# Ten quads of MLP down products as seven block products each, in a two-layer decoder trunk on one core

## The chip, the cores and the metric

The kernel runs on one core of a Trainium2 chip. The metric is the device time of one execution in microseconds. A profiled execution carries its own time beside its span (the time from the first to the last instruction that the profile holds).

## What is computed

The reference is a trunk of two layers on 512 tokens of width 1024, all in float32. In each layer the mixing part (attention, a short convolution, RWKV-7) comes first and is not touched here. Then comes the MLP:

```
h = rms_norm(x, norm_mlp_g[l])                              # x: (512, 1024)
x = x + square(relu(h @ w_mlp_up[l])) @ w_mlp_down[l]       # up: 1024 -> 4096, down: 4096 -> 1024
```

After the second layer there is a last norm. Only the MLP's two products matter below.

## The kernel before

Activations lie transposed, feature rows on the 128 partitions and the 512 tokens in the free dimension; `x[0..7]` are the eight residual tiles of 128x512. Every float32 product is made of three passes on TensorE (PE): each operand is split into a high part (a rounded copy, cast by ScalarE, ACT) and a low part (the difference, a subtraction on VectorE, DVE, or GpSimd, POOL), and the passes are high·high, low·high and high·low. So each weight tile costs one load, one cast on ACT (`whi`, `shi`) and one subtraction on DVE (`wlo`, `slo`).

**Up.** The up product has 32 groups of 128 hidden columns. Four (`up`) are plain. The other 28 go in 14 calls of `two(i0, i1)`, each of which makes two groups with seven block products in place of eight, by a scheme of the Strassen-Winograd kind: weights are cut into blocks of 4x128 rows, tokens into halves of H = 256, and four sums of weight blocks (`s1` to `s4`, DVE), four sums of activation blocks (`th`, made once in a layer by `blocks`) and a few sums of results replace one product. One product is 4 blocks by 3 passes, 12 matmuls of 256 columns. Results lie in PSUM banks `pa`, `pb`, `pc`; ACT copies some out (`p1`, `p5`, `u2`, `c1`), DVE adds. `square` makes the hidden tile (relu times the token's norm, then the square), and `kept` splits it into `mh` (ACT) and `ml` (POOL, from the fifth tile on) and adds it to the list `mids`.

**Down.** `down(h, js)` multiplies four hidden tiles (index h, 0 to 7) by the weights of four output tiles j (js is 0 to 3 or 4 to 7): per j 4x3 = 12 matmuls of 512 columns into a bank `dn`, and an addition of the bank to `x[j]` on DVE. `weights` loads, casts and subtracts; it has three sets of buffers in the pool `wp`, and every fourth tile uses a set in `fp` (`spare`).

The loop over p = 0 to 13 calls `two`, and as soon as four tiles more are there, one `down` of four products. So the steady state is an alternation of one `two` and one `down` of four j, called a unit below. The order of instructions on each engine is made by a list scheduler when the program is built; each engine then works in that order, and waits where an operand or a buffer isn't ready.

In layer 0 all of h = 0 to 7 goes through `down`; in layer 1 h = 6 and 7 go through `last_group`.

Of the kernel before, what the change touches and what calls it, by code (L numbers as in the profile page):

```python
# [22 lines left out]
S = 512  # L23
# [159 lines left out]

WHOLE = 5
# [87 lines left out]
def tile_trunk(ctx: ExitStack, tc: tile.TileContext, xT, wts, prm_d, cst_d, lora_d, gup_d, lam_d, fin_d, hd_d, out):  # L272
# [46 lines left out]
    fixed = cp.tile([P, 9], F32, tag="ones1", name="ones1")  # L319
# [246 lines left out]
    for l in range(L):  # L566
# [826 lines left out]
        with ExitStack() as mx:  # L1393
            fp = mx.enter_context(tc.tile_pool(name=f"fp{l}", bufs=1))
            spare[0] = fp
# [6 lines left out]
            def kept(m):  # L1402

                i = len(mids)
                hi = fp.tile([P, S], F32R, tag="mh", bufs=RING, name=f"mh{l}_{i}")
                lo = fp.tile([P, S], F32R, tag="ml", bufs=RING, name=f"ml{l}_{i}")
                act.copy(hi, m)  # L1407
                (dve if i < 4 else pool).tensor_tensor(lo, m, hi.bitcast(F32), ALU.subtract)  # L1408
                mids.append((hi, lo))

            def square(cs, name):

                r = fp.tile([P, S], F32, tag="r", bufs=2, name=f"r{name}")
# [5 lines left out]
                kept(m)  # L1419

# [25 lines left out]
            def blocks(q):  # L1446
                hi, lo = th[q] = [fp.tile([P, 4, H], F32R, tag=f"t{p}{q}", name=f"t{p}{l}_{q}") for p in ("hi", "lo")]
                for i in range(2):
                    u = slice(2 * i, 2 * i + 2)
                    t = fp.tile([P, 2, H], F32, tag="c0" if q == 1 else ("s3", "s4")[i], bufs=1 + (q == 1), name=f"t{l}_{q}_{i}")  # L1450
                    for k in (2 * i, 2 * i + 1):
                        b1, b2, o = bn[k], bn[k + 4], t[:, k % 2]
                        if q == 0:
                            dve.tensor_tensor(o, b1[:, 1], b1[:, 0], ALU.subtract)
                        elif q == 1:
                            dve.tensor_tensor(o, b2[:, 1], tb[0, i][:, k % 2], ALU.subtract)
                        elif q == 2:
                            dve.tensor_tensor(o, b2[:, 1], b1[:, 1], ALU.subtract)
                        else:
                            dve.tensor_tensor(o, b2[:, 0], tb[1, i][:, k % 2], ALU.subtract)  # L1460
                    tb[q, i] = t
                    act.copy(hi[:, u], t)
                    dve.tensor_tensor(lo[:, u], t, hi[:, u].bitcast(F32), ALU.subtract)

            def two(i0, i1):
# [4 lines left out]
                def raw(i, a):  # L1470
                    t = fp.tile([P, 4, P], F32, tag="sraw", bufs=6, name=f"raw{n}_{i}_{a}")
                    nc.sync.dma_start(t.rearrange("p k c -> p (k c)"), wts[wg + i, :, a * P:(a + 4) * P])
                    return t
# [7 lines left out]
                def sum_(name, a, b, op):  # L1481
                    t = fp.tile([P, 4, P], F32, tag=name, name=f"{name}{n}")
# [27 lines left out]
                w21 = raw(i1, 0)  # L1510
                w22 = raw(i1, 4)
                s1 = sum_("s1", w21, w22, ALU.add)
# [3 lines left out]
                s2 = sum_("s2", s1, w11, ALU.subtract)  # L1516
# [3 lines left out]
                w12 = raw(i0, 4)  # L1520
                product(pc, both(w12, "p2"), blk(1, 0))
                dve.tensor_tensor(c0[:, :H], pc, p1, ALU.add)
                s3 = sum_("s3", w11, w21, ALU.subtract)
# [4 lines left out]
                s4 = sum_("s4", w12, s2, ALU.subtract)  # L1528
                product(pb, both(s4, "p3"), blk(1, 1), False)
                dve.tensor_tensor(c0[:, H:], pb, u2, ALU.add)  # L1530
                square([c0], f"{n}_0")
                product(pa, both(w22, "p4"), smm(3), False)
                square([pa, c1], f"{n}_1")

            def down(h, js):

                g, k0 = h // 2, 4 * (h % 2)
# [29 lines left out]
            for p in range(N_TWO):  # L1567
                two(N_ONE + p, N_ONE + N_TWO + p)
                if len(mids) >= 4 * h + 6 and h < 2 * N_KG - 2 * (l == L - 1):
                    down(h, range(4 * half, 4 * half + 4))  # L1570
                    h, half = h + half, 1 - half
            while h < 2 * N_KG - 2 * (l == L - 1):
                down(h, range(4 * half, 4 * half + 4))
                h, half = h + half, 1 - half
# [71 lines left out]
```

## Time and profile before

| | us |
|---|---|
| median of 3 runs | 1236.49 (1235.99 to 1236.52) |
| profiled execution, its own time | 1238.42 |
| its span | 1236.6 |
| PE busy | 1226.2 (99%) |
| DVE busy | 934.4 (76%) |
| ACT busy | 693.0 (56%) |
| POOL busy | 351.7 (28%) |
| TensorE clock granted | 0.998 of full |

The profiled execution took 1.93 us more than the median, and its span is 1.8 us shorter than its own time. "Busy" is the time in which an engine had at least one instruction in work. The share of PE is nearly the whole span, so what matters is how far the matmuls stand apart in a stage, and which wait would come last there if PE had less to do.

### The profile page before, as it was taken

What the parts mean: (1) busy time and instruction counts of PE and PEld (TensorE: products, weight loads), DVE (VectorE), ACT (ScalarE), POOL (GpSimd) and SP (SyncE); (2) the same over time, 40 slices, a digit from 0 to 9 for tenths busy, and PEclk for the clock granted to TensorE, in tenths of its full rate; (3) what the DMA queues carried; (4) which work ended last, traced back from release to release, by engine and by line L of the source; (5) the groups of instructions that cost most, each with busy time, mean ns of one, the idle gap of its engine ahead of it and who ended that gap; (6) DMA issues with size and microseconds to landing.
All of it is one profiled execution on the core that took longest, in us unless ns stands there. A gap on an engine that the chain in (4) does not pass through costs nothing.

```text
span 1236.6 us, 25555 instructions
## 1 busy us (share of the span) xinstructions
PE 1226.2 (99%) x9730; PEld 1056.4 (85%) x9730; DVE 934.4 (76%) x1805; ACT 693.0 (56%) x1456; POOL 351.7 (28%) x450
## 2 busy tenths in 40 slices
PE   9999999999999999999999999999999999999997
PEld 7788788888999998989888888888889999998987
DVE  6787888879887676765666777887798867676753
ACT  6785655558455454544465657464775545454542
POOL 2263636341122111120035455464202211111111
PEclk9999999999999999999999999999999999999999
DMA  6523323124433323321235243232433333323121
GB/s 217 165 91 96 111 90 111 54 86 154 143 97 102 103 94 107 99 86 44 69 105 166 77 126 114 88 85 70 152 113 118 106 102 102 104 95 107 55 69 68
DMA packets 84266, 127.94 MB, mean 103 GB/s; under 512 B 21296, under 2 KB 25136, under 8 KB 84144
## 3 DMA queue, kind: packets, MB, share of 16 engines
q1 hardware_dynamic: 83424, 125.57, 32.5%
q8 instruction: 76, 1.25, 0.4%
q10 hardware_dynamic: 720, 0.75, 0.2%
q14 instruction: 46, 0.38, 0.1%
HBM read 117.11 MB, written 9.18 MB: 102 GB/s over the span
## 4 chain that ended last, share of the span: by engine, by line
PE 92%; DVE 2%; ACT 2%; DMA 1%; POOL 1%; issue 1%; SPq 0%; POOLq 0%; ACTq 0%; DVEq 0%
PE dn L285 25%; PE pj L285 21%; PE pa L285 13%; PE po L285 8%; PE pb L285 7%; PE dnF L285 4%; PE pc L285 3%; PE up L285 2%; PE sc L285 1%; PE ptt L290 1%; PE pg L285 1%; PE pyy L285 1%; PE pzw L285 1%; PE pst L285 1%; DMA raw<-wts 0%
## 5 line engine op out<-in xcount | busy, mean ns | idle before, releaser
L1408 POOL TENSOR_TENSOR ml<-m,mh 128x512 fp32r<-128x512 f32 x56 | 90.5, 1634 | 497.5 <-ACT mh L1407 356.5
L285 PE MATMUL dn<-mh,whi 128*128 128x512 f32 x448 | 175.5, 392 | 0.0
L285 PE MATMUL dn<-ml,whi 128*128 128x512 f32 x448 | 175.2, 391 | 0.1
L285 PE MATMUL dn<-mh,wlo 128*128 128x512 f32 x448 | 175.2, 391 | 0.0
L692 POOL TENSOR_TENSOR wlo<-raw,whi 128x512 fp32r<-128x512 f32 x84 | 111.5, 1328 | 210.4 <-ACT whi L680 167.2
L346 ACT CAST whi<-raw 128x512 fp32r<-128x512 f32 x126 | 77.9, 619 | 157.5 <-PE dn L285 147.8
L285 PE MATMUL pj<-ahim,whi 128*128 128x512 f32 x392 | 156.8, 400 | 0.0
L285 PE MATMUL pj<-ahim,wlo 128*128 128x512 f32 x392 | 156.4, 399 | 0.0
L285 PE MATMUL pj<-alom,whi 128*128 128x512 f32 x392 | 155.9, 398 | 0.0
L1554 DVE TENSOR_TENSOR x<-dn,x 128x512 f32<-128x512 f32 x108 | 74.5, 690 | 89.9 <-PE dn L285 89.8
L680 ACT CAST whi<-raw 128x512 fp32r<-128x512 f32 x142 | 87.7, 618 | 71.7 <-PE pj L285 27.5
L1477 ACT CAST shi_p<-s 128x512 fp32r<-128x512 f32 x112 | 69.4, 621 | 78.4 <-PE pa L285 61.9
L347 DVE TENSOR_TENSOR wlo<-raw,whi 128x512 fp32r<-128x512 f32 x126 | 97.3, 774 | 6.1 <-ACT whi L346 6.1
L285 PEld LDWEIGHTS dn<-mh,wlo 128*128 128x128 f32 x448 | 84.2, 188 | 18.5
L285 PEld LDWEIGHTS dn<-ml,whi 128*128 128x128 f32 x448 | 84.2, 188 | 17.7 <-DVE ml L1408 0.5
L285 PEld LDWEIGHTS dn<-mh,whi 128*128 128x128 f32 x448 | 84.1, 188 | 17.4
L285 PE MATMUL pa<-thi,shi_p 128*128 128x256 f32 x336 | 95.1, 283 | 0.0
L285 PE MATMUL pa<-tlo,shi_p 128*128 128x256 f32 x336 | 94.9, 282 | 0.0
L285 PE MATMUL pa<-thi,slo_p 128*128 128x256 f32 x336 | 94.1, 280 | 0.0
L1478 DVE TENSOR_TENSOR slo_p<-s,shi_p 128x512 fp32r<-128x512 f32 x112 | 77.6, 697 | 21.2 <-ACT shi_p L1477 18.4
L285 PEld LDWEIGHTS pj<-alom,whi 128*128 128x128 f32 x392 | 73.9, 188 | 14.0 <-issue 0.5
L285 PEld LDWEIGHTS pj<-ahim,wlo 128*128 128x128 f32 x392 | 73.8, 188 | 13.9 <-issue 0.2
(427 smaller groups left out, 3242.5 us busy)
## 6 DMA issues: line engine op xcount, KB each, us to landing
raw<-wts SPq DMA_DIRECT2D x389, 256.0 KB, 2.6
qs<-dqhi SPq DMA_DIRECT2D x24, 128.0 KB, 3.4
ks<-dkhi SPq DMA_DIRECT2D x24, 128.0 KB, 3.6
x<-xT SPq DMA_DIRECT2D x8, 256.0 KB, 5.0
dqhi<-qhi SPq DMA_DIRECT2D x6, 256.0 KB, 3.4
dqlo<-qlo SPq DMA_DIRECT2D x6, 256.0 KB, 3.4
dkhi<-khi SPq DMA_DIRECT2D x6, 256.0 KB, 3.1
dklo<-klo SPq DMA_DIRECT2D x6, 256.0 KB, 3.5
```

What stands on the lines that cost most here:

```text
L285: ins = nc.tensor.matmul(*a, **k)
L290: ins = nc.tensor.transpose(*a, **k)
L346: act.copy(hi[:, :n], raw[:, :n])
L347: (pool if a and lean[0] else dve).tensor_tensor(lo[:, :n], raw[:, :n], hi[:, :n].bitcast(F32), ALU.subtract)
L680: yield act.copy(hi[:, k0:k1], raw[:, k0:k1])
L692: yield eng.tensor_tensor(lo[:, k0:k1], raw[:, k0:k1], hi[:, k0:k1].bitcast(F32), ALU.subtract)
L1408: (dve if i < 4 else pool).tensor_tensor(lo, m, hi.bitcast(F32), ALU.subtract)
L1477: act.copy(hi, src)
L1478: dve.tensor_tensor(lo, src, hi.bitcast(F32), ALU.subtract)
L1554: dve.tensor_tensor(x[j], pt, x[j], ALU.add)
```

## The change

**Quads.** A table names ten (h, half) pairs, six in layer 0 (h = 2, 4, 6, both halves) and four in layer 1 (h = 2, 4). For these, `quad` replaces the four plain down products. It takes the four outputs as two pairs of j and makes each pair by seven block products: each is 2 blocks of 128 rows by 3 passes, 6 matmuls of 256 columns. The weight sums `s2q`, `s4q` are made on DVE from two loads in each pair, and four parts are split (`whi`/`wlo` a and d, `shi`/`slo` b and c). Results go to banks `qa`, `qb`, `qc`; ACT copies `p1q`, `p5q`, `u2q`, `c1q` out, DVE makes `c0q`, `c1q` and adds to `x`. The sums of hidden blocks that the scheme needs are made by `turn_blocks` after the `two` that makes the hidden tiles: six additions or subtractions of 256 columns and one of 512 on DVE, one wide and two narrow casts on ACT.

**Weight sums by adding loads.** In `two` for p = 1 to 13, `s1` and `s3` are not made on DVE any more. `summed` loads one addend into the tile from SP's queue, and then a second load from POOL's queue adds to it in place (`accum_op`). Signs are turned so that all sums are additions; the second half's relu becomes a `min` with 0 before the square.

**The rest.** Plain down products alternate between two banks `mm` and two of the four `rp`; the fourth weight set (`spare`) is gone; `square` works in place; some pools change their number of buffers.

```diff
+DN_QUADS = (((2, 0), (2, 1), (4, 0), (4, 1), (6, 0), (6, 1)), ((2, 0), (2, 1), (4, 0), (4, 1)))
...
-            spare[0] = fp
...
-            def square(cs, name):
+            def square(cs, name, side=ALU.max):
...
-                    dve.scalar_tensor_tensor(r[:, q], c, 0.0, rs[:, q], ALU.max, ALU.mult)
-                m = fp.tile([P, S], F32, tag="m", bufs=3, name=f"m{name}")
-                act.activation(m, r, AF.Square)
+                    dve.scalar_tensor_tensor(m[:, q], c, 0.0, rs[:, q], side, ALU.mult)
+                act.activation(m, m, AF.Square)
...
+            def summed(p, name):
+
+                if p < N_TWO:
+                    i0, i1 = N_ONE + p, N_ONE + N_TWO + p
+                    t = sums[p, name] = fp.tile([P, 4, P], F32, tag=name, bufs=2, name=f"{name}{l}_{i0}")
+                    of = [wts[wbase + NG_IN + NG_OUT + i, :, a * P:(a + 4) * P] for i, a in ((i1, 0), (i1, 4) if name == "s1" else (i0, 0))]
+                    nc.sync.dma_start(t.rearrange("p k c -> p (k c)"), of[0])
+                    pool.dma_start(t.rearrange("p k c -> p (k c)"), of[1], accum_op=ALU.add)
...
+            def turn_blocks(h, k, b1, b2):
+
+                a = fp.tile([P, 2, H], F32, tag="c0", bufs=2, name=f"ta{l}_{h}_{k}")
+                b = fp.tile([P, 2, H], F32, tag="c0", bufs=2, name=f"tb{l}_{h}_{k}")
+                dve.tensor_tensor(a[:, 0], b1[:, H:], b1[:, :H], ALU.subtract)
+                dve.tensor_tensor(a[:, 1], b2[:, H:], a[:, 0], ALU.subtract)
+                dve.tensor_tensor(b[:, 0], b2[:, H:], b1[:, H:], ALU.subtract)
+                dve.tensor_tensor(b[:, 1], b2[:, :H], a[:, 1], ALU.subtract)
+                hi, lo = [fp.tile([P, 2, H], F32R, tag=f"d{p}{k}", name=f"d{p}{l}_{h}_{k}") for p in ("hi", "lo")]
+                act.copy(hi, a)
+                dve.tensor_tensor(lo, a, hi.bitcast(F32), ALU.subtract)
...
+            def quad(h, half):
...
+                for i in range(2):
...
+                    w0 = split(r0, wp, ("whi", "wlo"), WB, f"{j}a")
+                    s = [fp.tile([P, 4, P], F32, tag=t, name=f"{t}q{n}") for t in ("s2", "s4")]
+                    dve.tensor_tensor(s[0][:, :2], r1[:, 0::2], r1[:, 1::2], ALU.add)
+                    dve.tensor_tensor(s[0][:, 2:], s[0][:, :2], r0[:, 0::2], ALU.subtract)
+                    s12 = split(s[0], fp, ("shi", "slo"), 5, f"{j}b")
+                    dve.tensor_tensor(s[1][:, :2], r0[:, 0::2], r1[:, 0::2], ALU.subtract)
+                    dve.tensor_tensor(s[1][:, 2:], r0[:, 1::2], s[0][:, 2:], ALU.subtract)
+                    s34 = split(s[1], fp, ("shi", "slo"), 5, f"{j}c")
+                    w22 = split(r1[:, 1::2], wp, ("whi", "wlo"), WB, f"{j}d")
...
+                for step in ((0, 1), (2, 3), (5, 4), (6,)):
+                    for j, w0, s12, s34, w22, (pa, pb, pc) in ab:
...
+                            elif c == 4:
+                                product(pa, s34, (0, 1), trn(2), False, False)
+                                c1 = copied("c1", pa, n)
+                                dve.tensor_tensor(c1, c1, keep["p5", j], ALU.add)
+                                add(j + 1, right, c1)
+                            else:
+                                product(pa, w22, (0, 1), trn(3), False, True)
+                                add(j + 1, left, pa)
...
             def down(h, js):
 
+                if (h, js[0] // 4) in DN_QUADS[l]:
+                    quad(h, js[0] // 4)
+                    return
...
-                    pt = psum("mm", 2, f"dn{l}_{h}_{j}")
+                    pt = psum(*(("mm", 2), ("rp", 4))[j % 2], f"dn{l}_{h}_{j}")
```

Where instructions moved: three places. PE in layer 0, where the plain products of h = 2, half 0 ended and the next `two` (number 9) began; `pa` is its first bank.

```order
L285 MATMUL dn_2_3_5480<-mh_11_5176,whi_0_5483 128x512
L285 MATMUL dn_2_3_5480<-ml_11_5177,whi_0_5483 128x512
L285 MATMUL dn_2_3_5480<-mh_11_5176,wlo_0_5484 128x512
L285 MATMUL pa_9_5500<-ahif_0_3860,shi_9_p_5506 128x256
L285 MATMUL pa_9_5500<-alof_0_3861,shi_9_p_5506 128x256
```

The same place in the changed kernel, where the last products of the quad stand:

```order
L287 MATMUL qa_2_0_5466<-ahif_3_3940,wlo_2_0d 128x256
L287 MATMUL pa_9_5612<-ahif_0_3860,shi_9_p_5618 128x256
L287 MATMUL pa_9_5612<-alof_0_3861,shi_9_p_5618 128x256
L287 MATMUL qa_2_2_5495<-ahif_1_3889,whi_2_2d 128x256
L287 MATMUL qa_2_2_5495<-alof_1_3890,whi_2_2d 128x256
L287 MATMUL qa_2_2_5495<-ahif_1_3889,wlo_2_2d 128x256
L287 MATMUL qa_2_2_5495<-ahif_3_3940,whi_2_2d 128x256
L287 MATMUL qa_2_2_5495<-alof_3_3941,whi_2_2d 128x256
L287 MATMUL qa_2_2_5495<-ahif_3_3940,wlo_2_2d 128x256
L287 MATMUL pa_9_5612<-ahif_0_3860,slo_9_p_5619 128x256
```

Two matmuls of the next `two` now stand between the last product of the first pair and that of the second.

DVE in layer 0, at the end of the down products of h = 2, half 1, before; `slo_10` and `slo_11` are weight parts of the next two calls of `two`:

```order
L1554 TENSOR_TENSOR x_73<-dn_2_5_5680,x_73 128x512
L347 TENSOR_TENSOR wlo_4_5924<-raw_4_5921,whi_4_5923 128x512
L1554 TENSOR_TENSOR x_74<-dn_2_6_5700,x_74 128x512
L347 TENSOR_TENSOR wlo_4_5944<-raw_4_5941,whi_4_5943 128x512
L1554 TENSOR_TENSOR x_75<-dn_2_7_5720,x_75 128x512
L347 TENSOR_TENSOR wlo_4_5964<-raw_4_5961,whi_4_5963 128x512
L1478 TENSOR_TENSOR slo_10_p_5851<-s_10_5848,shi_10_p_5850 128x512
```

And now, at the end of the quad:

```order
L1644 TENSOR_TENSOR c0q_2_4_5842<-qb_2_4_5797,u2q_2_4_5874 128x256
L1491 TENSOR_TENSOR slo_10_p_5987<-s_10_5984,shi_10_p_5986 128x512
L1595 TENSOR_TENSOR x_72<-c0q_2_4_5842,x_72 128x512
L1649 TENSOR_TENSOR c1q_2_4_5906<-c1q_2_4_5906,p5q_2_4_5866 128x256
L1644 TENSOR_TENSOR c0q_2_6_5858<-qb_2_6_5826,u2q_2_6_5890 128x256
L1595 TENSOR_TENSOR x_73<-c1q_2_4_5906,x_73 128x256
L1595 TENSOR_TENSOR x_74<-c0q_2_6_5858,x_74 128x512
L1649 TENSOR_TENSOR c1q_2_6_5924<-c1q_2_6_5924,p5q_2_6_5882 128x256
L1595 TENSOR_TENSOR x_73<-qa_2_4_5796,x_73 128x256
L1595 TENSOR_TENSOR x_75<-c1q_2_6_5924,x_75 128x256
L1595 TENSOR_TENSOR x_75<-qa_2_6_5825,x_75 128x256
L1491 TENSOR_TENSOR slo_10_p_6015<-raw_10_10_4_6004,shi_10_p_6014 128x512
```

The low part of the fourth weight tile of `two` number 10 (`slo_10_p_6015`) now stands behind nine additions of the quad.

POOL in layer 0, early in the MLP, before, where only the low parts of hidden tiles stand:

```order
L1408 TENSOR_TENSOR ml_4_4512<-m_4_0_4509,mh_4_4511 128x512
L1408 TENSOR_TENSOR ml_5_4537<-m_4_1_4534,mh_5_4536 128x512
L1408 TENSOR_TENSOR ml_6_4752<-m_5_0_4749,mh_6_4751 128x512
L1408 TENSOR_TENSOR ml_7_4777<-m_5_1_4774,mh_7_4776 128x512
L1408 TENSOR_TENSOR ml_8_4912<-m_6_0_4909,mh_8_4911 128x512
```

And now, with the adding loads among them:

```order
L1409 TENSOR_TENSOR ml_4_4513<-m_4_0_4509,mh_4_4512 128x512
L1409 TENSOR_TENSOR ml_5_4537<-m_4_1_4532,mh_5_4536 128x512
L1476 DMA s_7_4847<-wts 128x512
L1476 DMA s_8_5096<-wts 128x512
L1409 TENSOR_TENSOR ml_6_4751<-m_5_0_4747,mh_6_4750 128x512
L1409 TENSOR_TENSOR ml_7_4775<-m_5_1_4770,mh_7_4774 128x512
L1476 DMA s_8_5099<-wts 128x512
L1476 DMA s_9_5348<-wts 128x512
```

Two adding loads stand ahead of each two low parts; the loads of `s_8` serve the `two` that comes three calls after the one whose tiles are `m_5`.

## Rows read from the trace of the kernel before

**Rows 1.** The page's span and its busy time of each engine.

```profile
span 1236.6 us, 25555 instructions
PE 1226.2 (99%) x9730; PEld 1056.4 (85%) x9730; DVE 934.4 (76%) x1805; ACT 693.0 (56%) x1456; POOL 351.7 (28%) x450
```

**Rows 2.** The chain that ended last, by engine and by line.

```profile
PE 92%; DVE 2%; ACT 2%; DMA 1%; POOL 1%; issue 1%; SPq 0%; POOLq 0%; ACTq 0%; DVEq 0%
PE dn L285 25%; PE pj L285 21%; PE pa L285 13%; PE po L285 8%; PE pb L285 7%; PE dnF L285 4%; PE pc L285 3%; PE up L285 2%; PE sc L285 1%; PE ptt L290 1%; PE pg L285 1%; PE pyy L285 1%; PE pzw L285 1%; PE pst L285 1%; DMA raw<-wts 0%
```

**Rows 3.** Timeline of PE (start, length, instruction): first matmul of three stages, each layer.

```profile
417.57 0.40 PE L285 MATMUL dn<-mh,whi 128*128 128x512 f32 x1
...
428.61 0.28 PE L285 MATMUL pa<-ahif,shi_p 128*128 128x256 f32 x1
...
438.61 0.40 PE L285 MATMUL dn<-mh,whi 128*128 128x512 f32 x1
...
1025.18 0.40 PE L285 MATMUL dn<-mh,whi 128*128 128x512 f32 x1
...
1036.11 0.28 PE L285 MATMUL pa<-ahif,shi_p 128*128 128x256 f32 x1
...
1046.11 0.40 PE L285 MATMUL dn<-mh,whi 128*128 128x512 f32 x1
```

**Rows 4.** Busy time of one unit: length, PE, PEld, DVE, ACT, POOL, clock, DMA.

```profile
407.57:428.61 21.04, 21.04 (x133) 19.02 (x132) 15.29 (x25) 10.12 (x20) 3.35 (x2) 1.00 0.32 99
```

**Rows 5.** Groups by line and shape: count, busy us, mean ns of one.

```profile
L1478 DVE TENSOR_TENSOR slo_p<-s,shi_p 128x512 fp32r<-128x512 f32 x112 | 77.6, 697 | 21.2 <-ACT shi_p L1477 18.4
...
L1486 DVE TENSOR_TENSOR s<-raw,raw 128x512 f32<-128x512 f32 x52 | 42.3, 818 | 1.3
...
L1477 ACT CAST shi_p<-s 128x512 fp32r<-128x512 f32 x112 | 69.4, 621 | 78.4 <-PE pa L285 61.9
```

**Rows 6.** Timeline of DVE over a stretch without idle time.

```profile
372.67 0.69 DVE L1486 TENSOR_TENSOR s<-raw,raw 128x512 f32<-128x512 f32 x1
...
375.86 0.69 DVE L1416 SCALAR_TENSOR_TENSOR r<-c,rsf 128x512 f32<-128x512 f32 x1
376.46 0.42 DVE L1416 SCALAR_TENSOR_TENSOR r<-pa,rsf 128x256 f32<-128x256 f32 x1
376.79 0.42 DVE L1416 SCALAR_TENSOR_TENSOR r<-c,rsf 128x256 f32<-128x256 f32 x1
377.12 0.69 DVE L1478 TENSOR_TENSOR slo_p<-s,shi_p 128x512 fp32r<-128x512 f32 x1
...
379.06 1.19 DVE L347 TENSOR_TENSOR wlo<-raw,whi 128x512 fp32r<-128x512 f32 x1
```

**Rows 7.** Timelines of DVE and of POOL over one stretch.

```profile
324.81 2.39 DVE L1486 TENSOR_TENSOR s<-raw,raw 128x512 f32<-128x512 f32 x2
327.12 0.68 DVE L1554 TENSOR_TENSOR x<-dn,x 128x512 f32<-128x512 f32 x1
...
325.02 3.34 POOL L1408 TENSOR_TENSOR ml<-m,mh 128x512 fp32r<-128x512 f32 x2 [35.10 <-ACT mh L1407]
```

**Rows 8.** Timelines of ACT and PE around the first copy of one `two`.

```profile
493.23 0.62 ACT L1477 CAST shi_p<-s 128x512 fp32r<-128x512 f32 x1 [0.91 <-PE pa L285]
493.75 0.37 ACT L1509 COPY p<-pa 128x256 f32<-128x256 f32 x1
...
493.15 0.28 PE L285 MATMUL pb<-thi,shi_p 128*128 128x256 f32 x1
...
494.58 0.28 PE L285 MATMUL pa<-thi,shi_p 128*128 128x256 f32 x1
```

**Rows 9.** Loads of weights (count, size, us to landing); POOL's timeline, its idle time.

```profile
raw<-wts SPq DMA_DIRECT2D x389, 256.0 KB, 2.6
...
483.26 1.65 POOL L1408 TENSOR_TENSOR ml<-m,mh 128x512 fp32r<-128x512 f32 x1 [17.70 <-PE dn L285]
```

**Rows 10.** Timeline of ACT: a cast of down weights and what it waited for.

```profile
491.69 0.62 ACT L346 CAST whi<-raw 128x512 fp32r<-128x512 f32 x1 [2.10 <-PE dn L285]
```

More of the change, by code (lines that the diff above doesn't have):

```diff
@@ L318, in tile_trunk @@
     bo2 = cst[:, K_BO2:K_BO2 + 2]
-    fixed = cp.tile([P, 9], F32, tag="ones1", name="ones1")
+    fixed = cp.tile([P, 3], F32, tag="ones1", name="ones1")
     ones1, mhalf, gn_eps = [fixed[:, i:i + 1] for i in range(3)]
@@ new lines, in quad, with split, product, add @@
+            def quad(h, half):
+                g, k0 = h // 2, 4 * (h % 2)
+                def split(src, pool_, tags, bufs, name):
+                    hi, lo = [pool_.tile([P, 4, P], F32R, tag=t, bufs=bufs, name=f"{t}{l}_{h}_{name}")[:, :src.shape[1]] for t in tags]
+                    act.copy(hi, src)
+                    dve.tensor_tensor(lo, src, hi.bitcast(F32), ALU.subtract)
+                    return hi, lo
+                def product(pt, w, ks, moving, first, last):
+                    for i, k in enumerate(ks):
+                        ahi, alo = moving(i)
+                        whi, wlo = [t[:, k] for t in w]
+                        pe.matmul(pt, whi, ahi, start=first and i == 0, stop=False, skip_group_check=True)
+                        pe.matmul(pt, whi, alo, start=False, stop=False, skip_group_check=True)
+                        pe.matmul(pt, wlo, ahi, start=False, stop=last and i == 1, skip_group_check=True)
+                blk = lambda d, q: lambda i: [t[:, q * H:(q + 1) * H] for t in mids[4 * h + 2 * i + d]]
+                trn = lambda q: lambda i: turned[q, i]
+                def add(j, q, pt):
+                    dve.tensor_tensor(x[j][:, q], pt, x[j][:, q], ALU.add)
+                def copied(name, pt, n):
+                    t = fp.tile([P, H], F32, tag=name, bufs=2, name=f"{name}q{n}")
+                    act.copy(t, pt)
+                    return t
+                left, right = slice(0, H), slice(H, S)
+                keep = {}
+                ab = []
+                for i in range(2):
+                    j = 4 * half + 2 * i
+                    n = f"{l}_{h}_{j}"
+                    r0, r1 = [wp.tile([P, 4, P], F32, tag="raw", bufs=WB, name=f"rawq{n}_{c}") for c in range(2)]
+                    for c, r in enumerate((r0, r1)):
+                        nc.sync.dma_start(r.rearrange("p k c -> p (k c)"),
+                                          wts[wbase + NG_IN + NG_OUT + NG_UP + 8 * g + j + c, :, k0 * P:(k0 + 4) * P])
+                    w0 = split(r0, wp, ("whi", "wlo"), WB, f"{j}a")
[7 more added lines that the diff above has]
+                    w22 = split(r1[:, 1::2], wp, ("whi", "wlo"), WB, f"{j}d")
+                    pts = [psum(t, b, f"q{c}{n}")[:, :H] for c, t, b in zip("abc", (("rp", "rp", "at"), ("mm", "mm", "at"))[i],
+                                                                          ((4, 4, 2), (2, 2, 2))[i])]
+                    ab.append((j, w0, s12, s34, w22, pts))
+                for step in ((0, 1), (2, 3), (5, 4), (6,)):
+                    for j, w0, s12, s34, w22, (pa, pb, pc) in ab:
+                        n = f"{l}_{h}_{j}"
+                        for c in step:
+                            if c == 0:
+                                product(pa, w0, (0, 2), blk(0, 0), True, False)
+                                keep["p1", j] = copied("p1", pa, n)
+                            elif c == 1:
+                                product(pc, w0, (1, 3), blk(1, 0), True, True)
+                                keep["c0", j] = c0 = fp.tile([P, S], F32, tag="c0", bufs=2, name=f"c0q{n}")
+                                dve.tensor_tensor(c0[:, left], pc, keep["p1", j], ALU.add)
+                            elif c == 2:
+                                product(pb, s12, (0, 1), trn(0), True, False)
+                                keep["p5", j] = copied("p5", pb, n)
+                            elif c == 3:
+                                product(pa, s12, (2, 3), trn(1), False, False)
+                                keep["u2", j] = copied("u2", pa, n)
+                            elif c == 5:
+                                product(pb, s34, (2, 3), blk(1, 1), False, True)
+                                c0 = keep["c0", j]
+                                dve.tensor_tensor(c0[:, right], pb, keep["u2", j], ALU.add)
+                                add(j, slice(0, S), c0)
+                            elif c == 4:
[3 more added lines that the diff above has]
+                                add(j + 1, right, c1)
+                            else:
+                                product(pa, w22, (0, 1), trn(3), False, True)
+                                add(j + 1, left, pa)
@@ L1571, in tile_trunk @@
                     h, half = h + half, 1 - half
+                hk = divmod(N_ONE // 2 + p, 2)
+                if any(q[0] == hk[0] for q in DN_QUADS[l]):
+                    turn_blocks(*hk, *ms)
             while h < 2 * N_KG - 2 * (l == L - 1):
```

45 lines of the change are left out of this document (29 added, 16 removed).

## Prediction

> **What bounds the kernel now.** First the busy times [rows 1]: PE is busy for 1226.2 of 1236.6 us, DVE for 934.4, ACT for 693.0, POOL for 351.7. Then the chain of waits [rows 2]: PE holds 92% of it, and the largest entries are the plain down products `dn` with 25% and the up products in `pa`, `pb`, `pc` with 23% together. So time is lost only where PE has something to do, and the question for each edit is whether it shortens PE's own row of matmuls or makes PE wait. Last the stage itself. A unit of the MLP is one half of a down and one `two`. PE's timeline [rows 3] gives the half down of layer 0 from 417.57 to 428.61, 11.04 us for 48 matmuls of 512 columns, and the `two` from 428.61 to 438.61, 10.00 us for 84 matmuls of 256 columns, 119 ns each. In layer 1 the half down runs from 1025.18 to 1036.11, 10.93 us, and `two` again takes 10.00. Over one unit [rows 4] PE works for 21.04 of 21.04 us at a granted clock of 1.00, DVE for 15.29, ACT for 10.12, POOL for 3.35, and the DMA engines for 0.32 of the time. DVE has 5.7 us to spare in a unit, and that is the number which the change spends.
>
> **What the quads take from PE.** A quad is 2 pairs x 7 products x 6 matmuls = 84 matmuls of 256 columns, the row of one `two`: 10.00 us. Against the plain half it gives 11.04 - 10.00 = 1.04 us six times and 10.93 - 10.00 = 0.93 us four times: 6.24 + 3.72 = 9.96 us. The condition is that weights are loaded under matmuls of 256 columns, which `two` shows in the same trace.
>
> **What it adds on DVE, and the adding loads.** I count a unit with a quad from the code. Wide instructions (512 columns): in `two` seven `slo`, the sums `s2` and `s4`, one first half of `square` over `c`, `p` of full width, together 10; in the quad, for each of two pairs, `wlo` of a, `slo` of b and c and one addition to `x`, 8; together 18. Narrow ones (256 columns): 5 in `two` and 20 in the quad (for each pair four half sums, `wlo` of d, two `c0q`, one `c1q`, two additions to `x`), together 25. Now the price. In a stretch without idle time [rows 6] the wide ones start 0.60 us apart and the narrow ones 0.33 (376.46, 376.79, 377.12), although 0.69 and 0.42 are listed, since an instruction begins before the one ahead of it has ended. At the pitch a unit costs 18 x 0.60 + 25 x 0.33 = 19.05 us; at the listed lengths 18 x 0.69 + 25 x 0.42 = 22.9. The same stretch from 372.67 to 379.06 holds 8 wide and 4 narrow ones, 6.12 at the pitch, and took 6.39: a factor of 1.044, so 19.9. POOL adds to it: while POOL makes `ml` (325.02 to 328.36) two sums of DVE take 2.39 us together [rows 7], 1.19 each, against 0.60. In the 3.35 us of POOL in a unit about three instructions with two inputs fall, each 0.55 us longer, at most 1.65. Half of that gives D = 20.7 us, all of it 21.5, for DVE's work in a unit with a quad, against PE's 20.0. Without the adding loads it would be two sums more, 2 x 0.60: D = 21.9. These sums had the mean of 818 ns listed [rows 5], 52 of them; they are what the loads take away. The seven `slo` of a `two` stay.
>
> The Trainium skill ("SBUF — State Buffer", "Who interferes with whom") says of a DVE instruction with two SBUF inputs beside a GpSimd instruction that reads SBUF that the shared port pair is an exclusive lock and the other fully blocks. By that DVE would stand for POOL's whole 3.35 us. Rows 7 speak for half speed: two sums got through in 2.39 us of POOL's 3.34. What the full block would give is a rival below.
>
> **Where DVE's surplus goes.** DVE stays behind by D - 20.0 in each unit with a quad. The quads come in five pairs of consecutive units, and between the pairs stand units with a plain down, in which DVE, with `turn_blocks`, has 19 wide and 11 narrow instructions: 15.0 us at the pitch, 16.7 with all of POOL's cost, against 21.0. So DVE enters each pair with its queue drained, as far ahead as the buffers let it. I followed the queues row by row through one pair of quads; the latest operand is the one at the end of the second quad, `slo` of the fourth weight tile of `two` number 10, which stands on DVE behind nine additions. At D = 20.7 it comes 0.5 us before PE asks for it. So the lead is 2 x 0.7 + 0.5 = 1.9 us, and the wait of PE for a pair of quads is S = 2 (D - 20.0) - 1.9, where that is positive: nothing at 20.7, 1.1 us at 21.5, 3.9 us at 22.9. The lead itself is uncertain by half a microsecond. I take 0.5 us for each pair, 5 x 0.5 = 2.5 us, since D's middle shows nothing and its upper half 1.1. Bounds: 0 and 5 x 3.9 = 19.5.
>
> **ACT's copies.** In a quad the last use of `qa` must wait until ACT has copied `c1q` from it, and before it `u2q` and `p1q`. In `two` PE's first matmul after the product in `pa` starts at 493.15, ACT casts from 493.23 and copies from 493.75 for 0.37 us [rows 8]: the copy ends 0.97 us after PE has left the bank, and PE comes back at 494.58, 1.43 us after leaving. In the quad the two pairs alternate, so that a product (6 x 0.119 = 0.71) or two stand between; at the last step of the second pair it is the 6 matmuls of the first pair and two of the next `two`, 8 x 0.119 = 0.95 us. So 0.02 us are open if ACT has one cast ahead, 0.5 if two, nothing if none. I take 0.1 for each of ten quads, 1.0 us; bounds 0 and 5.
>
> **Loads and buffers.** A `two` after the first one fetches two sums by two loads each, one from SP and one adding load from POOL. The trace of before holds no load that POOL issues, so POOL's share and the adding itself are bounded. POOL stands idle for 17.70 us ahead of an `ml` [rows 9], so a microsecond or two for an issue costs nothing; where the issue waits for SP's load, which lands after 2.6 us, `ml` behind it waits too. The narrowest place is layer 0's start, where two adding loads stand ahead of `ml_6` and `ml_7`; the down of h = 1 needs them 11.4 us after the `two` that makes them ends (one more `two` and the half down of h = 0), and two `ml` take 3.34 us. That leaves 8 us for two loads in a row with a price of 2.6 or twice that each. The sums are fetched a unit or more ahead of need. I take 0; bounds 0 and 3 us a layer. The DMA engines go from 8 to 11 loads of 256 KB in such a unit, 0.32 to some 0.43 [rows 4]. The fourth weight set is gone: a cast of down weights then waits until the product three before it is over. Today a cast already waits 2.10 us for PE [rows 10], and it starts two products, 5.5 us, ahead of its use, for a cast of 0.62 and a subtraction of 0.69. Nothing. The alternation of `dn` over `mm` and `rp` gives a bank longer rest than before and costs nothing, since the addition to `x` takes 0.68 [rows 7] and PE returns a product of 2.7 us later at the earliest. The signs and the in-place square change no count.
>
> **The sum.** -9.96 + 2.5 + 1.0 + 0 = -6.5 us. The profiled execution took 1238.42 (span 1236.6) and should go to 1231.9; it stood 1.93 above the median of 1236.49, and I keep that distance: **1230.0 us**.
>
> **Rivals.**
> *Given back.* Nothing need fail: D = 21.6 (all of POOL's cost) gives S = 2 x 1.6 - 1.9 = 1.3 for a pair, 6.5 us, and with 1.0 for ACT the gain is 2.5; with S = 1.8 it is zero, with 2.3 it is 2.5 us lost. 1234 to 1239. For it speaks that DVE has hardly any slack for two units on end; against it, that `ml` overlaps partly with narrow additions from PSUM, which at 327.12 took 0.68 beside POOL [rows 7], no longer than elsewhere.
> *DVE becomes the bound, slower.* At the end of each second quad PE waits for `slo`. It decides from 5 S = 9.96 - 1.0, S = 1.79, D = 21.85. The listed lengths give 22.9. At D = 22.65, the pitch of 19.05 with half of the way to the listed lengths (21.0) and all of POOL's cost, S is 3.4, 17 us in all: 1236.49 - 9.96 + 1.0 + 17 = 1244.5. For it: semaphore waits between narrow instructions that depend on each other (four half sums in a row, `c1q` and its addition) may leave the pitch for the listed length. Against it: rows 6 show narrow ones at 0.33 in a row of three.
> *Full block.* If DVE stood for all of POOL's `ml`, 3.35 us in a unit, D = 19.05 + 3.35 = 22.4, S = 2.9, 14.5 us: 1242. That is the rule of the Trainium skill named above; the sums of rows 7 that got through speak against it.
> *Adding loads come late.* If an adding load takes 10 us or holds POOL so long, `ml_6` and `ml_7` or a `shi` of a sum come late at the head of each layer, 3 us a layer: 1236. Nothing in the trace prices it.
> *Quads do not run at 119 ns a matmul.* The row of `two` has the same shapes and as many weight loads; I give this no share of its own.
>
> **How the numbers follow.** The forecast (1226.5, no stall at all, to 1234) has 0.60; given back 0.16; DVE the bound 0.14; adding loads late 0.06; full block 0.04. A measurement of this kernel tells about 0.2%, 2.5 us, from no change: faster is below 1234.0, slower above 1239.0. Faster: 0.60, and 0.07 from the near ends of given back and of late loads: 0.67. Slower: 0.14 + 0.04 less 0.01: 0.17. The rest, 0.16, is the same. The range runs from 1226.3 (the 9.96 kept, and a little from relieved DVE in units without a quad) to 1241, which takes in given back and late loads and leaves out most of the two slower cases.
>
> **What would show it.** On PE in the trace of after, a quad should last 10.0 us and a `two` 10.0; a pair with no gap confirms the lead, a gap ahead of the last `slo` of the `two` in or after the second quad confirms the surplus, one ahead of the seventh product confirms ACT's copy. DVE's busy time in a unit with a quad should lie near 20; the narrow instructions should start 0.33 apart. A gap with POOL's load as its releaser at the head of a layer would price the adding loads. If PE shows no gap and the time is still above 1230, a quad's matmuls are longer than 119 ns, and the first term was wrong.

## The result and the profile after

The changed kernel takes 1239.4 us in the median of 9 runs (1236.63 to 1241.35), against 1236.52 for the kernel before in the same set: a ratio of 1.0019, 95% interval 1.001 to 1.0028. The forecast was 1230.0, in a range that ended at 1241.0, and faster. It came out some 3 us slower.

The profiled execution took 1238.0 us. Its page, span and busy times:

```profile
span 1236.2 us, 26900 instructions
PE 1217.8 (99%) x10090; PEld 1065.6 (86%) x10090; DVE 1011.3 (82%) x2023; ACT 742.6 (60%) x1606; POOL 386.0 (31%) x502
```

Against [rows 1] PE has 8.4 us less to do, and the span is only 0.4 us shorter. Even that is too kind. The first `up` of layer 0 begins at 278.48 us in the trace of before and at 275.92 here, and in every trace used below between 275.3 and 276.5, the nearly unchanged kernel before of `e8_before_banks` (276.12) among them. That start of before was 2.4 us late by itself. From there on the changed kernel takes 2.2 us more.

PE's timeline (start, length, instruction) gives the stages, as [rows 3] did. Two quads with their two `two`, and the plain half behind them:

```profile
394.34 0.28 PE L287 MATMUL qa<-mh,whi_0a 128*128 128x256 f32 x1
...
414.51 0.28 PE L287 MATMUL qa<-mh,whi_4a 128*128 128x256 f32 x1
...
436.88 0.39 PE L287 MATMUL dn<-mh,whi 128*128 128x512 f32 x1
...
447.76 0.28 PE L287 MATMUL pa<-ahif,shi_p 128*128 128x256 f32 x1
```

The first unit takes 20.17 us, nearly the 20.00 that its matmuls need. The second takes 22.37. The pair needs 42.54 where two units of before needed 42.08. The other pairs by the same reading: 43.04 in layer 0 (before 42.08), 42.68 and 42.92 in layer 1 (before 41.86). Only the last pair of layer 0, which no `two` follows, runs with 0.17 us of waits. So the four others wait 2.54, 3.04, 2.68 and 2.92 us. The plain half takes 10.88 us (the others 10.93), where layer 0 had 11.04.

Where PE waits in the first pair, in the same timeline; the bracket is the idle time ahead of the instruction and what ended it:

```profile
420.21 0.39 PE L287 MATMUL qa<-dhi,shi_6b 128*128 128x256 f32 x1 [0.53 <-ACT p1q L1599]
...
424.18 0.39 PE L287 MATMUL qa<-ahif,whi_4d 128*128 128x256 f32 x1 [0.15 <-ACT c1q L1599]
...
435.34 0.39 PE L287 MATMUL pa<-thi,shi_p 128*128 128x256 f32 x1 [0.91 <-ACT c L1545]
```

Matmuls overlap in this view, so more is lost than the bracket says. From start to start the three places cost 0.79, 0.41 and 1.17 us above the pitch of 0.119, the wait at the end of the first quad 0.18: 2.55 in all. Each time ACT had not yet copied a bank. Why it had not at the first place stands a few rows further up. First ACT's timeline, then DVE's, then SP's queue:

```profile
416.06 0.62 ACT L1579 CAST shi_6b<-s2q 128x512 fp32r<-128x512 f32 x1 [3.83 <-DVE s2q L1615]
...
419.79 0.37 ACT L1599 COPY p1q<-qa 128x256 f32<-128x256 f32 x1
```

```profile
409.60 0.42 DVE L1617 TENSOR_TENSOR s4q<-rawq,rawq 128x256 f32<-128x256 f32 x1
409.94 0.42 DVE L1618 TENSOR_TENSOR s4q<-rawq,s2q 128x256 f32<-128x256 f32 x1
...
412.41 0.42 DVE L1546 TENSOR_TENSOR c<-c,p 128x256 f32<-128x256 f32 x1
414.88 0.43 DVE L1614 TENSOR_TENSOR s2q<-rawq 128x256 f32<-128x256 f32 x1 [2.05 <-DMA rawq<-wts]
```

```profile
410.05 0.33 SPq L343 DMA_DIRECT2D raw<-wts  x1
410.42 0.43 SPq L1610 DMA_DIRECT2D rawq<-wts  x1
```

DVE stood idle for 2.05 us, for a load of raw weights. SP issued it at 410.42, when DVE had ended at 410.36 the last reading (`s4q`, L1618) of the first pair's first tile: a quad loads four tiles, and the ring `raw` has three buffers. The load landed 4.4 us later, with three others in flight (the 40 loads `rawq` have a median of 2.9 over the whole execution). The issues of 408 to 416 us, by kind: count, size, us to landing:

```profile
raw<-wts SPq DMA_DIRECT2D x2, 256.0 KB, 4.1
rawq<-wts SPq DMA_DIRECT2D x1, 256.0 KB, 4.4
s<-wts POOLq DMA_DIRECT2D x1, 256.0 KB, 4.9
```

So DVE could go on at 414.88. By my estimate some 1.5 of the 2.05 us are the slow landing: at the median of 2.9 the load would have been there at 413.3, and DVE stood from 412.83. ACT, in order, stood idle for 3.83 us before the cast of that sum, and its copies for PE stood behind. The other second quads show the same: idle times of 1.70, 2.19 and 2.45 us on DVE at the same line, for loads that took 4.0 to 4.8 us.

DVE never gets these 2 us back, and so `c` at 435.34 comes late too. ACT's copy `c` stands behind the cast of a sum for the next `two`, and DVE ended that sum at 434.28, 0.11 us before the cast began. The bracket names PE; in `e1_raw4` the bracket of the same cast names DVE's `s`. DVE and ACT:

```profile
433.59 0.69 DVE L1499 TENSOR_TENSOR s<-s,raw 128x512 f32<-128x512 f32 x1
...
434.39 0.62 ACT L1490 CAST shi_p<-s 128x512 fp32r<-128x512 f32 x1 [2.22 <-PE pb L287]
434.92 0.37 ACT L1545 COPY c<-pa 128x256 f32<-128x256 f32 x1
```

The busy times of the three units (columns as in [rows 4]) say how full DVE is:

```profile
384.34:404.52 20.18, 20.18 (x170) 20.06 (x169) 18.22 (x36) 14.04 (x31) 2.97 (x2) 1.00 0.27 93
404.52:425.70 21.18, 20.50 (x170) 20.09 (x169) 19.13 (x38) 13.88 (x31) 4.98 (x4) 1.00 0.47 123
425.70:446.90 21.20, 20.30 (x131) 18.38 (x130) 21.20 (x41) 11.20 (x23) 6.10 (x6) 1.00 0.71 193
```

DVE worked 19.13 of 21.18 us in the second, all but the 2.05, and every bit of the third.

A fifth wait stands in layer 0 ahead of the quads, 0.85 us from start to start. PE waits for ACT's copy `p`, and ACT had stood before a cast for a load of down weights. PE, ACT, SP's queue, and the landing times of the issues from 357.8 to 359:

```profile
366.16 0.39 PE L287 MATMUL pa<-thi,shi_p 128*128 128x256 f32 x1 [0.58 <-ACT p L1522]
...
364.70 0.62 ACT L348 CAST whi<-raw 128x512 fp32r<-128x512 f32 x1 [3.75 <-DMA raw<-wts]
...
358.81 0.33 SPq L343 DMA_DIRECT2D raw<-wts  x1
...
s<-wts POOLq DMA_DIRECT2D x1, 256.0 KB, 6.5
raw<-wts SPq DMA_DIRECT2D x1, 256.0 KB, 5.8
```

The load took 5.8 us beside an adding load of POOL that took 6.5. More on it stands with `e9_plain_pool_load`.

### The profile page after: what moved, and what is told of

Read it like the earlier page. It is cut to its first block, busy times and chain, and to the rows that moved or that the text cites. A ratio compares the mean times of both kernels' runs of the same rounds, so it can differ in the third digit from the quotient of the medians.

```text
span 1236.2 us, 26900 instructions
## 1 busy us (share of the span) xinstructions
PE 1217.8 (99%) x10090; PEld 1065.6 (86%) x10090; DVE 1011.3 (82%) x2023; ACT 742.6 (60%) x1606; POOL 386.0 (31%) x502
## 5 line engine op out<-in xcount | busy, mean ns | idle before, releaser
L1476 POOL DMA_DIRECT2D s<-wts x52 | 48.0, 922 | 293.3 <-DVE slo_p L1491 68.5
L1409 POOL TENSOR_TENSOR ml<-m,mh 128x512 fp32r<-128x512 f32 x56 | 82.3, 1518 | 178.9 <-ACT mh L1408 63.1
L682 ACT CAST whi<-raw 128x512 fp32r<-128x512 f32 x142 | 87.6, 618 | 70.3 <-PE pj L287 26.5
L287 PE MATMUL dn<-mh,whi 128*128 128x512 f32 x288 | 112.3, 390 | 0.0
L287 PE MATMUL dn<-ml,whi 128*128 128x512 f32 x288 | 112.2, 390 | 0.0
L287 PE MATMUL dn<-mh,wlo 128*128 128x512 f32 x288 | 112.1, 390 | 0.0
L348 ACT CAST whi<-raw 128x512 fp32r<-128x512 f32 x86 | 52.9, 620 | 56.2 <-PE dn L287 30.7
L287 PEld LDWEIGHTS pj<-ahim,whi 128*128 128x128 f32 x392 | 73.8, 188 | 13.7 <-issue 0.3
L349 DVE TENSOR_TENSOR wlo<-raw,whi 128x512 fp32r<-128x512 f32 x86 | 72.5, 846 | 10.7 <-ACT whi L348 10.7
L1490 ACT CAST shi_p<-raw 128x512 fp32r<-128x512 f32 x84 | 52.4, 624 | 33.6 <-PE pb L287 18.1
L287 PEld LDWEIGHTS pa<-thi,shi_p 128*128 128x128 f32 x336 | 63.0, 188 | 6.1 <-ACT c L1545 4.7
```

The costliest lines, as they stand in the source:

```text
L287: ins = nc.tensor.matmul(*a, **k)
L348: act.copy(hi[:, :n], raw[:, :n])
L349: (pool if a and lean[0] else dve).tensor_tensor(lo[:, :n], raw[:, :n], hi[:, :n].bitcast(F32), ALU.subtract)
L682: yield act.copy(hi[:, k0:k1], raw[:, k0:k1])
L1476: pool.dma_start(t.rearrange("p k c -> p (k c)"), of[1], accum_op=ALU.add)
L1490: act.copy(hi, src)
```

## The experiments

Theory A was now: the fourth raw load of a second quad comes late for want of a buffer. Rival B: DVE has more work than the units have time. Rival C: the adding loads crowd POOL and the queues. Ratios are to the kernel before, run on the same chip.

**A fourth raw buffer.**

```diff
-r0, r1 = [wp.tile([P, 4, P], F32, tag="raw", bufs=WB, ...) for c in range(2)]
+r0, r1 = [(fp.tile([P, 4, P], F32, tag="raw4", ...) if (i, c) == (1, 1) else
+           wp.tile([P, 4, P], F32, tag="raw", bufs=WB, ...)) for c in range(2)]
-m = fp.tile([P, S], F32, tag="m", bufs=4, name=f"m{name}")
+m = fp.tile([P, S], F32, tag="m", bufs=3, name=f"m{name}")
```

> The changed kernel with one more buffer for the raw weights of a quad: its fourth load (the second tile of the second pair) has a buffer of its own and no longer waits until s4q of the first pair has read the tile three loads before. To make room, the tiles m have 3 buffers in place of 4. Theory A (the fourth load comes late because of its buffer; in the second quad of each of four pairs DVE idles some 2 us for it, ACT 3.8 us behind, and PE waits twice, 2.5 to 3.0 us for a pair in all): the waits at qa in the second quad and at pa in the two after it go, 4 x 2.7 = 10.8 us, median 1239.4 - 10.8 = 1228.6 us (1227 to 1231). Rival B (DVE simply has more than 20 us of work in a unit with a quad): the idle time of DVE goes but PE still waits at the end of each pair; 1236 or more. Rival C (the adding loads crowd the queues and POOL): no more than 2 us gained, 1237.5 or more.

1232.26 us, ratio 0.9962 (0.9949 to 0.9975): 7.1 below the changed kernel. No instruction of DVE waits for `rawq` any more, and a pair takes 40.95 or 40.96 us. DVE and PE at the place of the old wait:

```profile
412.49 0.41 DVE L1615 TENSOR_TENSOR s2q<-rawq 128x256 f32<-128x256 f32 x1
...
418.53 0.39 PE L287 MATMUL qa<-dhi,shi_4b 128*128 128x256 f32 x1 [0.35 <-ACT p1q L1599]
```

One wait of 0.63 us (from start to start) is left in each pair, and some 0.2 at `c1q` in each quad; the one at `c` of the next `two` is gone. So theory A holds for the larger part: all waits in quads come to 4.2 us in this trace, against 11.35 in the changed kernel. It is not the whole: 1228.6 was expected. DVE's busy time in the four units from the first quad on shows that it is full in the second and nearly so in the plain one behind:

```profile
384.28:404.37 20.09, 20.09 (x169) 19.97 (x168) 18.37 (x35) 14.08 (x31) 3.25 (x2) 1.00 0.30 93
404.37:425.16 20.79, 20.44 (x171) 20.12 (x170) 20.79 (x43) 14.17 (x31) 5.08 (x4) 1.00 0.56 152
425.16:446.15 20.99, 20.99 (x134) 19.08 (x134) 20.71 (x39) 11.18 (x22) 6.06 (x6) 1.00 0.73 176
446.15:467.08 20.93, 20.93 (x133) 19.01 (x132) 17.58 (x32) 11.26 (x22) 4.87 (x4) 1.00 0.53 140
```

The control has only the smaller number of buffers for `m`:

> Control for e1_raw4: the changed kernel with 3 buffers for the tiles m in place of 4 and nothing else. Theory A: as the changed kernel, 1239.4 us, the same waits in the second quad of each pair. If the buffers of m were what e1_raw4 gained by, 1233.

1237.94 us, ratio 1.0007 (0.9998 to 1.0015). That is 1.5 below the changed kernel in another set of runs, so up to that much of the 7.1 may belong to `m` or to the sets; the buffer for `raw` has the other 5.6. The cleanest pair comes below: `e3_dvesums` and `v3_m4` differ by the raw buffer alone, 1237.78 against 1232.66 us (ratios 1.001 and 0.9964, from two sets).

**The change without its quads.** `DN_QUADS = ((), ())`.

> The changed kernel with an empty table of quads: all down products plain, no sums of hidden blocks; the adding loads, the four banks for dn and the missing fourth weight set stay. It prices the rest of the change by itself. Theory A: PE waits only at the head of a layer (0.85 us in one two of layer 0), and plain halves of layer 0 at 10.93 in place of 11.04 give back up to 16 x 0.11 = 1.8: 1235.5 us (1234 to 1237). Rival C (adding loads cost): 1239 or more.

1237.09 us, ratio 1.0004 (0.9996 to 1.0013), just above theory A's range and short of rival C's 1239. Adding loads, banks and buffers by themselves give nothing, though plain halves of layer 0 take 10.93 us. One place where it is lost is the first half down of layer 1, 11.81 us there (11.25 before). PE waits for a hidden tile's low part:

```profile
910.58 0.50 PE L287 MATMUL dn<-ml,whi 128*128 128x512 f32 x1 [0.24 <-DVE ml L1409]
```

**Quads with sums on DVE**, from two plain loads, in all calls of `two`:

```diff
-if i0 == N_ONE:
-    w21, w22 = raw(i1, 0), raw(i1, 4)
-    s1 = sum_("s1", w21, w22, ALU.add)
-else:
-    s1 = sums[i0 - N_ONE, "s1"]
+w21, w22 = raw(i1, 0), raw(i1, 4)
+s1 = sum_("s1", w21, w22, ALU.add)
```

> The changed kernel with its ten quads, but the sums s1 and s3 made on DVE for every two, from two plain loads, as in the kernel before; no adding loads, 6 buffers for the raw tiles of two. Theory A: the fourth load of a quad is still late by its buffer, and DVE has two sums more (1.2 us a unit): waits of 3 to 5 us for a pair, 1240 to 1247 us. Rival B: D rises from about 20.4 to 21.6 us, S by 2.4 for a pair: 1249 us. Rival C: faster than the changed kernel, 1236 or less.

1237.78 us, ratio 1.001 (1.0001 to 1.0018). Neither A's 1240 to 1247 nor B's 1249, nor C's 1236. DVE has 1.2 us more work in each unit (two sums at 0.60), and the pairs wait 2.36, 3.60, 2.21 and 2.95 us, on the mean as before (2.78 against 2.80). Rival B falls as the cause of the changed kernel's loss: more work on DVE only fills the time in which it stood waiting for the load (0.53 us is left of 2.05 at this place):

```profile
413.67 0.42 DVE L1607 TENSOR_TENSOR s2q<-rawq 128x256 f32<-128x256 f32 x1 [0.53 <-DMA rawq<-wts]
```

**Single quads**, the first of each pair: `DN_QUADS = (((2, 0), (4, 0), (6, 0)), ((2, 0), (4, 0)))`.

> The changed kernel with only the first quad of each pair: (2,0), (4,0), (6,0) in layer 0, (2,0), (4,0) in layer 1, so that a plain half down follows each quad. Theory A: no wait in these; PE saves 3 x 1.04 + 2 x 0.93 = 5.0 us on quads and up to 1.4 on plain halves of layer 0, less 0.85 at the head: 1231 us (1230 to 1233). Rival B gives the same, since DVE has a unit of slack after each quad. If a quad by itself gives nothing on PE, 1236.

1233.94 us, ratio 0.9978 (0.9968 to 0.9987). All five quads run without the long waits (20.16 us with their `two`), so a quad does give what PE's row says, but for 0.17 us at `c1q`. Of the 3 us above the forecast, 1.0 is one wait in layer 0: 1.84 us at the place of the changed kernel's 0.85, which the forecast had counted. Five times 0.17 make 0.8 more, and the time behind layer 1's last `two` is 1.0 longer than in the trace of before, with no cause that I can name.

**Four buffers and sums on DVE:** the edits of `e1_raw4` and `e3_dvesums` together.

> e1_raw4 (quads with a fourth raw buffer, m with 3 buffers) with s1 and s3 made on DVE from plain loads in place of adding loads. It asks what the adding loads are worth once the quad's loads come in time. Theory A with DVE now near its bound (20.8 of 20.8 us busy in the second quad's unit of e1_raw4): 1.2 us more DVE work in each of two units, S from 0.6 to 3.0 us for each of four pairs, 9.6 us, less about 1 us at the heads of the layers: 1240 us. Rival (DVE still has room; the adding loads cost as much on POOL and DVE as they take): 1231 to 1233 us.

1232.41 us, ratio 0.9962 (0.995 to 0.9974): the same as `e1_raw4`. The wait in a second quad grows from 0.63 to 1.36 us, so the adding loads do relieve DVE by 0.7 us a pair, 2.9 in four, where 9.6 was forecast. But without them the first half down takes 10.91 and 10.88 us in the two layers, with them (`e1_raw4`) 11.52 and 11.85, so 1.6 us of this are lost again. The other 1.3 are lost outside the MLP's units, where traces differ by as much without a known cause. With four buffers for `m`:

> e5_raw4_dvesums (four raw buffers, sums on DVE) with 4 buffers for the tiles m, for which the missing second buffers of s1 and s3 leave room. If the waits of 1.36 us in the second quad come from ACT's squares and casts of m, held by the third buffer of m, they shrink to 0.6 or less and the time goes to 1229.5; if m's buffers play no part, 1232.4 as there.

1232.66 us, ratio 0.9964 (0.9951 to 0.9976), and the same wait:

```profile
418.75 0.39 PE L287 MATMUL qa<-dhi,shi_4b 128*128 128x256 f32 x1 [1.10 <-ACT p1q L1592]
```

The buffers of `m` play no part here.

**Banks alone.** The kernel before, with `psum("mm", 2, ...)` for `dn` replaced by the alternation of `mm` and `rp`.

> The kernel before with one edit: plain down products alternate between the banks mm and rp. In the trace of before a plain half takes 11.04 us in layer 0 and 10.93 in layer 1; with the change 10.93 in both. If the banks are the reason: 10.93 in layer 0 and 16 x 0.11 = 1.8 us less, 1235.2. If the banks are without effect (another cause, as where the tiles lie): 11.04 and 1237.0.

1236.41 us, ratio 0.9997 (0.9988 to 1.0005). The half down of layer 0 still takes 11.04 us, so the banks are not what made it 10.93:

```profile
373.12 0.40 PE L285 MATMUL dn<-mh,whi 128*128 128x512 f32 x1
...
384.16 0.28 PE L285 MATMUL pa<-ahif,shi_p 128*128 128x256 f32 x1
```

**Adding or only loading.** `accum_op=ALU.add` taken from the load on POOL.

> The changed kernel whose second load from POOL does not add but overwrites (so the sums s1 and s3 are wrong from the second call on, and with them the output); every instruction, transfer and wait stays. In the changed kernel one DVE instruction of 2.6 to 3.9 us stands at each of the seven places where POOL makes ml right behind the issue of an adding load. If the issue itself beside ml is the cause, they stay, and the time is that of the changed kernel, 1239. If the adding is, they go, and the wait of 0.85 us in the head of layer 0 with them.

1237.01 us, ratio 1.0003 (0.9993 to 1.0013), so the adding itself may cost some 2 us; the interval overlaps that of the changed kernel. The kernel's sums `s1` and `s3` lack one addend. By section 6 of the two pages the load from POOL lands after 4.4 us in the changed kernel and after 3.1 here:

```profile
s<-wts POOLq DMA_DIRECT2D x52, 256.0 KB, 4.4
```

```profile
s<-wts POOLq DMA_DIRECT2D x52, 256.0 KB, 3.1
```

The wait of 0.85 us in layer 0 is gone. The load whose lateness made it is issued at 358.77 here, at 358.81 in the changed kernel, and lands after 4.3 us in place of 5.8:

```profile
raw<-wts SPq DMA_DIRECT2D x1, 256.0 KB, 4.3
```

In the other traces it goes the same way: the load takes 6.2 and 6.4 us where that wait is 0.82 and 1.84 (`v2_adds8`, `e4_single`), and 4.6 where there is none (`e1_raw4`). Why a load lands so late beside an adding one, the traces don't show.

The second question was where the long DVE instructions come from. In the changed kernel, POOL's and then DVE's timeline in the same stretch:

```profile
354.79 0.88 POOL L1476 DMA_DIRECT2D s<-wts  x1 [6.14 <-DVE ta L1561]
355.36 2.86 POOL L1409 TENSOR_TENSOR ml<-m,mh 128x512 fp32r<-128x512 f32 x2
```

```profile
355.30 3.49 DVE L349 TENSOR_TENSOR wlo<-raw,whi 128x512 fp32r<-128x512 f32 x1
358.71 0.41 DVE L1562 TENSOR_TENSOR tb<-m,m 128x256 f32<-128x256 f32 x1
```

One `wlo` takes 3.49 us, all the time in which POOL makes two `ml` right behind the issue. It lasts 2.64 to 3.85 us at all seven such places. Without the adding such an instruction stays at five of six places:

```profile
354.08 3.13 DVE L1499 TENSOR_TENSOR s<-s,raw 128x512 f32<-128x512 f32 x1
```

So the issue ahead of `ml` goes with the block, and not the adding. The block at 354.08 stands ahead of the place of the wait, as that at 355.30 does in the changed kernel, and PE doesn't wait: the block alone does not make it. The kernels without loads from POOL show no block. It is not bound to happen: in `e2_noquads` it is one place of three.

**Putting it together.** Four raw buffers, adding loads only for the calls of `two` in and behind a second quad; then also in the first.

```diff
+ADDS = (5, 6, 9, 10, 13)
-if p < N_TWO:
+if p in ADDS:
```

> e1_raw4 with adding loads only for the calls of two in and behind the second quad of a pair (p = 5, 6, 9, 10, 13); elsewhere s1 and s3 are made on DVE. Theory: adding loads help only where DVE is tight (0.7 us a pair between e5_raw4_dvesums and e1_raw4) and cost at the heads of the layers (0.6 and 0.9 us in the first half down of e1_raw4): both gains together, 1230 us (1229.5 to 1231.5). If adding loads cost the same wherever they stand, or the pairs wait as in e5_raw4_dvesums: 1232.

1230.25 us (1229.17 to 1231.13), ratio 0.9945 (0.9932 to 0.9959): 6.8 us below the kernel before, and with the next one the best here. No `ml` starts less than 0.7 us behind an issue, no instruction of DVE in the MLP's loop takes over 2 us, both first halves take 10.9 us, and a pair takes 40.97. POOL and DVE at one of the places:

```profile
435.20 0.89 POOL L1477 DMA_DIRECT2D s<-wts  x1 [15.75 <-DVE slo_p L1492]
437.18 3.60 POOL L1409 TENSOR_TENSOR ml<-m,mh 128x512 fp32r<-128x512 f32 x2 [1.08 <-PE dn L287]
```

```profile
438.44 1.19 DVE L349 TENSOR_TENSOR wlo<-raw,whi 128x512 fp32r<-128x512 f32 x1
439.55 1.51 DVE L1562 TENSOR_TENSOR ta<-m,ta 128x256 f32<-128x256 f32 x1
```

> As v1_adds5 with adding loads also for the two of the first quad of a pair (p = 4, 5, 6, 8, 9, 10, 12, 13): DVE has 1.2 us less work in that unit too, so the wait in the second quad should be that of e1_raw4 (0.63 us a pair) or less: 1230 us. If a wait of 1.36 stays, the wait isn't set by DVE's work in that unit.

1230.34 us, ratio 0.9944 (0.9931 to 0.9956). The three further adding loads a layer change nothing at the pairs (40.98 us), and bring back two long DVE instructions and a wait of 0.82 us in layer 0.

## Why the prediction was wrong

**PE's gain: right.** Every unit of a first quad shows 20.16 to 20.18 us. The 9.96 us are there, and 1.0 more, since plain halves left in layer 0 take some 0.11 less, which no step foresaw (eight of ten; a wait behind the last quad takes it back from the last two).

**The waits: the step that failed.** It is the sentence on loads and buffers: "The fourth weight set is gone: a cast of down weights then waits until the product three before it is over [...] Nothing." That was worked out for plain products, which load one tile each and free it as they go. A quad loads four tiles, all of them needed before its third product, and three buffers hold three; the first of them is free only when the last half sum of the first pair is made, and that stands on DVE behind the last additions of the quad before it and five low parts. Each of the four late loads then took 4.0 to 4.8 us, where [rows 9] had 2.6. I followed casts, subtractions and additions through the queues, but not the loads. The forecast for all waits in quads was 2.5 + 1.0 = 3.5 us. They come to 2.54 + 3.04 + 0.17 + 2.68 + 2.92 = 11.35. The difference of 7.85 us is most of the miss of 9.4, and one more buffer takes back 5 to 7 of it.

**DVE's work: near in size, wrong in place.** One unit does not show D, since DVE works ahead and behind. Over the four units shown for `e1_raw4`, two with a quad and two plain, it is busy for 77.4 us; two times 20.7 and two times 16.7 make 74.8. For a pair 0.5 us was taken (the formula itself gave nothing at 20.7), and 0.63 is left at `p1q` once the load comes in time. That these lie so near is luck: it is not the last `slo` of `two` 10 that comes late. DVE's lateness goes through ACT: `square`'s results come late, ACT's squares and casts stand ahead of the copy `p1q`, and PE waits for that. And the price of more DVE work, 2 us of waits for 1 us of work in each unit, was too high: the sums of `e5_raw4_dvesums` cost 0.73 for a pair and not 2.4.

**ACT's copies: right in kind, too small.** 0.1 us a quad was forecast; the `c1q` waits are 0.17 to 0.2 in a first quad and 0.41 in the second one shown.

**The adding loads: a cost put at nothing.** Their cost was put at 0 with a bound of 3 us a layer, their worth at 1.2 us of D. In the changed kernel they cost 0.85 us in one wait, by a plain load that landed after 5.8 us beside one, and `e2_noquads`, where nothing needs the relief, is no faster than before although its plain halves are shorter. Only where DVE is short do they pay, and from `e1_raw4` to `v1_adds5` 2.0 us come from taking the others out.

**Rivals.** "Given back", 1234 to 1239, is nearest in size, but by another cause than its own. "Adding loads come late" is a part of it, though what came late was a plain load beside one. "Given back" calls D = 21.6 all of POOL's cost, where the count gave 21.5; that is 0.2 us a pair. "Full block" was given 0.04 as a rule for all of POOL's `ml`. [rows 7] still show half speed there, and so do the 1.19 and 1.51 us of `v1_adds5`; right behind an issue the block is real at most places. The plain pitch was not the trouble: narrow instructions do start 0.33 us apart in the quads.

**The sum put right**, for the traces, from the start of layer 0's `up`: -9.96 on quads, -1.0 on plain halves of layer 0, +11.35 waits in quads, +0.85 at the head of layer 0, -0.1 in the first half down of layer 1, which leaves +1.1; 1.0 more lies outside the MLP's units (0.46 in layer 1's mixing part and 0.5 behind the last `two`), where the traces differ among themselves too, by 0.6 and 1.2 us. Together 2.1; the traces give 2.2.

With these two things mended (a fourth buffer, adding loads only where DVE is full) the change gives -6.8 us, about what was forecast for it as it stood.

What stays open: why a plain half of layer 0 takes 11.04 us in the kernel before and 10.93 in the changed ones (not the banks); the last 0.63 us a pair, which moved with DVE's work but was not tried by itself; and how much of the late fourth load is its late issue and how much its slow landing, since a buffer of its own mends both.

## What to carry to other kernels

Where an edit makes one step take several tiles of a ring of buffers at once, count the tiles against the buffers first, and ask which instruction frees the one that the last load needs, and where that stands in its queue. A queue of loads is followed row by row like any engine's: its wait shows on an engine two steps further on. Work moved from a full engine to another pays only at the places where the engine is full; elsewhere its cost remains.

## What the hardware showed

The block behind an issue was not expected. With POOL's `ml` alone, a DVE instruction of two inputs takes 1.19 us instead of 0.60 [rows 7], and DVE goes on. Where `ml` starts 0.57 us behind the issue of a POOL load, a DVE instruction took 2.64 to 3.85 us, at seven of seven places of the changed kernel. In `v1_adds5`, where an issue lies 2 us ahead of `ml`, it is 1.19 and 1.51 again. Over the changed kernel and the six experiments with loads from POOL (`e7_m3` aside), a DVE instruction took over 2 us at 29 of the 34 places with 0.55 to 0.62 us between issue and `ml`, and at none with 0.75 us or more. The Trainium skill ("SBUF — State Buffer", "Who interferes with whom") calls the shared port pair an exclusive lock that whoever issues first holds for the whole instruction. The seven places agree with that in length: at six of them the DVE instruction ended 0.55 to 0.57 us after POOL's second `ml`. They don't agree in which comes first, since at four it had started before the first `ml`. The half speed of [rows 7] does not agree at all, and the traces don't show what makes the difference beyond the issue that stands ahead.

A load from POOL that adds landed after 4.4 us in the median, the same load without adding after 3.1 (`e9_plain_pool_load`), a plain load of weights from SP after 2.8, all of 256 KB. One plain load, issued 0.95 us behind an adding one, took 5.8 us.
